# Expert weights in a two-block network: who makes the second parts of streamed weights, and how the spread weights lie in PSUM

## The chip, the cores and the metric

One core of one Trainium2 chip runs the whole program in one launch. The metric is device time in microseconds (us), the median of several runs. "PE" is TensorE, "DVE" VectorE, "ACT" ScalarE, "POOL" GpSimd, "SP" the engine whose queue issues most DMAs.

## The reference

The network takes 256 tokens of 1024 features through two layers of a first block (a mixer, then a layer of experts) and two layers of a second block (attention). The change lies in the experts. Each layer has 16384 experts; every token has 8 heads, each head picks 16 experts, and the output is the sum over the picked experts. Cut to that:

```python
def block(xb):
    q = (xb @ w_q).reshape(n, PEER_HEADS, 2, PEER_HALF)
    s = jnp.einsum('nhpc,pkc->nhpk', q, sk)
    sv, si = lax.top_k(s, PEER_TOPK)
    ...                                    # fv, eid: the 16 best pairs of each head
    gw = jax.nn.softmax(fv, axis=-1)
    u = u_tab[eid]
    act = jax.nn.gelu(jnp.einsum('nhkd,nd->nhk', u, xb), approximate=False)
    coef = gw * act
    return jnp.einsum('nhk,nhkd->nd', coef, v_tab[eid])
```

## The kernel before

**Dense experts.** The kernel gathers nothing. It computes the activation of every expert for every token (`u_pair`: gelu of u times x), multiplies it with a weight that is zero for experts that were not picked, and adds up all experts' outputs (`v_pairs`). Experts lie in 128 blocks of 128; a "pair" is two blocks and one DMA of 1 MB. The activations of 96 blocks lie in SBUF in three tiles `H[0]` to `H[2]`, each 128 partitions x 32 blocks x 256 tokens; they are a ring, so the u pairs and v pairs of `peer` are interleaved: u 0 to 47, v 0 to 7, u 48 to 55, v 8 to 15, u 56 to 63, v 16 to 63.

**Two parts of every number.** Weights are float32 and TensorE multiplies a shorter format (float32r). So `load_w` takes each 1 MB chunk `raw` in two halves: ScalarE copies a half to `whi` (line 122, the first part), and another engine subtracts `whi` from `raw` to make `wlo` (line 126, the second part). Each half then gives 24 products: 16 with `whi`, 8 with `wlo`. `whi` and `wlo` have 3 buffers each, `raw` has 3. The letter `lo` says which engine makes `wlo`: "p" GpSimd, "v" VectorE, "m" GpSimd for every third half and VectorE for the others.

**Spreading the weights.** `gates` takes 8 tokens and 64 blocks of experts at a time. A picked expert has a number within its block and a block number. VectorE compares both with a row of counts: `oh_b` (line 931, 128 x 1024 float16) and `oh_a` (line 934, 128 x 512), and multiplies `oh_a` with the softmax weights in two float16 parts: `oh_w` (line 938, two instructions). TensorE then makes, for each of the 8 tokens, `oh_b` times `oh_w` of both parts into 64 columns of a PSUM bank (line 942, 16 products of 64 columns), and VectorE multiplies the bank into two of the `H` tiles (line 949, two SCALAR_TENSOR_TENSOR instructions of 256 elements each). One call is made for each of 32 groups of tokens and each half of the blocks. The calls of the first half stand beside u pairs 32 to 46, those of the second beside v pairs 16 to 30, two calls (near the end three) to a pair. With two layers there are four such stages and 128 calls.

**Order.** A planner in the language's runtime orders the instructions of each engine from the order in which they are traced; waits between engines are semaphores that it places. `oh_b`, `oh_a` and `oh_w` have two buffers each, the PSUM banks named "tr" two. Side work for the second block (`beside`: lines 1065 to 1109, products of `w_ada` on VectorE) is spread over the experts' pairs too.

Of the kernel before, what the change touches and what calls it, by code (L numbers as in the profile page):

```python
# [20 lines left out]
P = 128  # L21
# [4 lines left out]
ALPHA = 4.0 ** 0.25  # L26
NEG = -1e30
LOWEST = -3.4e38
# the columns of a tile of tokens that are ready in turn
PIECES = (((0, 512), (512, 1024)), ((0, 512), (512, 768), (768, 1024)))  # L30
GATE_SCALE = 2.0 ** 14


def weave(main, fill, ratio):
    """Trace main, with ratio steps of fill to each of its own; then the rest of fill."""
    acc = 0.0
    for _ in main:
        acc += ratio
        while acc >= 1.0:
            next(fill, None)  # L40
            acc -= 1.0
    for _ in fill:
        pass
# [8 lines left out]
class Net:  # L52
# [8 lines left out]
    def new_T(self):  # L61
        """The slot of the features of the tokens: features on partitions, two parts."""
        return self.state.tile([P, KD, 2, S], F32R, name="xT", tag="xT", bufs=1)
# [13 lines left out]
    def consts(self, tmp):  # L77
# [5 lines left out]
        # row r, column c: NEG where c > r  # L83
# [12 lines left out]
    def mlstm_consts(self, c, d):  # L96
        """By row r and column k: 1 where r <= k; NEG where k < r; selectors of the heads' rows."""
# [10 lines left out]
    def load_w(self, src, width, nsub, lo="v", into=None):  # L108
        """The parts of a chunk of weights, of two products of the same columns; into: where to lay them."""
# [4 lines left out]
        parts = []  # L114
# [23 lines left out]
    def gemm_b(self, xT, chunk, ps, lo="m", KT=KD, fresh=False):  # L138
        """ps[:, 2, 256] <- (two blocks of 128 columns of W)^T x^T; a step is a block. fresh: x's
        second parts come last, in the first block."""  # L140
# [12 lines left out]
    def gemm_a(self, xT, chunks, ktc, w, evac, nsub=2, lo="m", ahead=False, tag="mm"):  # L153
        """evac(t, ps) with ps = x W for the two tiles of tokens, w columns; a step is a part of a
        chunk. ahead: the first tile's last products come before the second's."""
# [31 lines left out]
    def to_T(self, dst, t, src, k0, n, pin=False):  # L187
        """dst[:, k0:k0+n, hi|lo, tile t] <- src[:, t, blocks k0 to k0+n] transposed; pin: not
        ahead of what was traced before."""
        for k in range(k0, k0 + n, 4):  # L190
            m = min(4, k0 + n - k)
            self.split(*self.both(dst, t, k, m), self.turned(src[:, t], k, m, pin))
# [12 lines left out]
    def tokens_T(self, pool, dst, src, warm):  # L205
        """dst <- src transposed. The first tile's turn, which runs beside the second's norm, leaves
        VectorE alone."""
# [11 lines left out]
    def keep_warm(self, n):  # L219
        """Products that nobody reads, for a wait that would cost the tensor engine its clock."""  # L220
# [5 lines left out]
    def rstd(self, pool, var, eps, shape, more=None, before=None):  # L226
        """1 / sqrt(var + eps (+ more)): a first guess from the bits of the number, then a step of the
        third order and one of the second."""
# [19 lines left out]
        # 8 / 3 of the next guess, r (15 - 10 y + 3 y^2) / 8  # L248
# [6 lines left out]
    def refine_exp(self, e, sg):  # L255
        """e = exp(x) to float32's accuracy from the tables' exp(x) and sigmoid(x), x <= 0:
        one step towards e (1 - sg) = sg. sg is overwritten."""
# [13 lines left out]
    def stats(self, pool):  # L271
        """bn_stats of each piece of each tile of tokens."""
        return [pool.tile([P, len(PIECES[t]), 6], F32, name=f"ln_st{t}") for t in range(NT)]

    def layer_norm(self, pool, x, st, g, b):
        """x, one tile of tokens, in place; st: bn_stats of its pieces."""
# [4 lines left out]
        # (mean - x) g, so that the other factor is negative  # L281
# [9 lines left out]
    def add_norm(self, pool, x, t, i, ps, st, g, b, scale=ALPHA):  # L291
        """x <- scale x + ps, piece i of a tile of tokens; with the last piece the tile's norm."""
# [10 lines left out]
    def project(self, xT, src, order, evac, tags, store=None, late=3):  # L303
        """evac(t, i, ps) with ps = x W for a tile of tokens and piece i of the columns; src(n, i): the
        i-th half of W's rows, by blocks in this order, for 512 columns. The last products of a tile come
        together, of as many parts of W as late; three parts lie in the usual place, more in store."""
# [38 lines left out]
    def log1p_exp(self, pool, out, x, shape, tag):  # L345
        """out = log(1 + exp(x)), as max(x, 0) + 2 atanh(e / (2 + e)), e = exp(-|x|)."""
# [28 lines left out]
    def mem_kv(self, l, memT):  # L375
        """Keys of the memory, feature-major, and its values."""
# [10 lines left out]
    def feature_gemm(self, xT, chunk, dst, func=AF.Copy, scale=1.0, lo="m", fresh=False):  # L387
        """dst[:, 512] <- func(scale (two blocks of 128 columns of W)^T x^T)"""
# [53 lines left out]
    def mlstm(self, pool, x, xT, mixT, memT):  # L442
        nc, a = self.nc, self.a
        # gates
# [24 lines left out]
        # nB = -(running sum of the log forget gates); r = i - B  # L469
# [25 lines left out]
        # decay weights, transposed: [s, l]; columns: s0 x (l0, l1), s1 x l1  # L495
# [30 lines left out]
        # values (with a column of ones)  # L526
# [8 lines left out]
        # sigmoid(o) = (1 + tanh(o / 2)) / 2, with the norm's gain  # L535
# [17 lines left out]
        for c in range(2):  # L553
# [3 lines left out]
            if c:  # L557
                # beside the transposes of the first two heads
# [46 lines left out]
    def rglru(self, pool, own, xT, mixT):  # L605
# [34 lines left out]
        # softplus(-lam), times 4  # L640
# [22 lines left out]
        def recurrence():  # L663
            # sigmoid(z) = (1 + tanh(z / 2)) / 2
            for c in range(3):
# [12 lines left out]
                # 1 - a^2 = tanh(-log a) (1 + a^2); a half of its root  # L678
# [29 lines left out]
    def exp_neg(self, x, k, r):  # L708
        """x <- exp(x), x <= 0, on the vector engine alone: 2^k times a series in what is left.
        k and r are overwritten."""  # L710
# [23 lines left out]
    def peer(self, l, x1, beside, rate):  # L734
        """x1 <- layer_norm(ALPHA x1 + y); beside: steps that may run beside the products, at a rate
        for each pair of blocks."""
        nc, a, tc = self.nc, self.a, self.tc
        with ExitStack() as st:
            big = st.enter_context(tc.tile_pool(name=f"peer{l}", bufs=1, reuse_waits="tile"))
            # a ring of 96 blocks of experts' activations; the last two thirds are freed early  # L740
# [52 lines left out]
            if l:  # L793
                # the diagonals of the second block's gates
# [22 lines left out]
    def route(self, pool, H, l, xT, R):  # L817
        """The 16 experts of each head and token, and their weights, with the slots on partitions.
        What is needed here only lies in the part of H that is written last."""
# [53 lines left out]
        # softmax over the 16  # L873
# [9 lines left out]
        # the two halves of the expert's number  # L883
# [27 lines left out]
    def u_pair(self, l, xT, H, c):  # L911
        ps = self.bank("aux")
        yield from self.gemm_b(xT, self.a["u"][l, c], ps, "p" if c < 14 or 32 <= c < 48 else "m")
# [6 lines left out]
    def gates(self, pool, R, H, half, n):  # L920
        """H[64 blocks of this half, 8 tokens] *= the experts' weights, as two float16 parts,
        which carry all of float32's bits: the weights lie in 0..1, and are scaled away from the smallest.
        Tokens lie in pairs, so that all operands run through memory in steps of one."""
# [15 lines left out]
        g = self.bank("tr")  # L939
        for t in range(8):  # L940
            for k in range(2):
                i = nc.tensor.matmul(g[:, t * 64:(t + 1) * 64], B[:, t // 2, :, t % 2], W[:, k, t // 2, :, t % 2],  # L942
# [3 lines left out]
        gv = g.rearrange("p (t i) -> p t i", t=8)  # L946
        for i0, hh in ((0, H[2 * half]), (32, H[1 - half])):
            h = hh[:, :, ts].rearrange("p i t -> p t i")
            nc.vector.scalar_tensor_tensor(out=h, in0=gv[:, :, i0:i0 + 32], scalar=1.0 / GATE_SCALE, in1=h,  # L949
                                           op0=OP.mult, op1=OP.mult)  # L950

    def v_pairs(self, pool, l, H, c0, c1):
        """y += the experts' outputs, two blocks of experts in a step."""
        for c in range(c0, c1):
            ch, cl = (pool.tile([P, 2 * S], F32R, name=n, tag=n, bufs=2) for n in ("ch", "cl"))
            self.split(ch, cl, self.h_pair(H, c))
            parts = self.load_w(self.a["v"][l, c], 2048, 2, "p" if 16 <= c < 32 else "v" if c >= 48 else "m")
# [6 lines left out]
    def v_products(self, t, out, first, last, b, ch, cl, hi, lw):  # L964
        """out: (first and last column, where) of each part."""
# [8 lines left out]
    def v_tail(self, pool, l, H, c0, done):  # L974
        """The last experts' outputs, tile by tile, from operands that are all laid ready; the steps lay
        them, a pair of blocks each. done(t, ys) with the sums of those before,
        done(t, y, i) with what piece i adds."""
# [44 lines left out]
    def load_T(self, pool, name, dst, parts):  # L1022
        """Features on partitions from DRAM, in two parts."""
# [8 lines left out]
    def bias_tables(self, pool):  # L1032
        """Rows of bias over distance, written 128 times, so that a pitch of one less skews them."""
# [19 lines left out]
    def bias_ap(self, h, off):  # L1053
        """The three groups' biases of a head for queries off tiles after the keys."""
# [4 lines left out]
    def rope_tables(self, pool):  # L1059
        """cos and sin of positions * inv_freq, by token."""  # L1060
# [29 lines left out]
    def modulation(self, pool, l, thirds):  # L1090
        """By feature: the shift, norm_g (1 + scale) and a half of the gate."""
# [22 lines left out]
    def gate_rows(self, l):  # L1114
        """The gate along the free dimension, on all partitions. Returns what is still to be done."""
# [10 lines left out]
    def rms_of(self, pool, ms):  # L1126
        """1 / sqrt(mean(x^2) + eps); the mean is the sum of ms' columns."""
# [7 lines left out]
    def rms(self, pool, srcs, tag):  # L1135
        """1 / sqrt(mean(x^2) + eps) of each of srcs, [P, len(srcs)]."""
# [12 lines left out]
    def second_layer(self, l, x, stats):  # L1149
        """x <- x + ..., and the result after the last layer; stats: the mean squares of x's pieces by  # L1150
        tile, or None. Returns those of the new x."""
        nc, a, tc = self.nc, self.a, self.tc
        mod = self.mods[l]
        with ExitStack() as st:
# [36 lines left out]
            # latents of the second mixer  # L1191
# [5 lines left out]
            # twice silu(z) = z (1 + tanh(z / 2))  # L1197
# [26 lines left out]
            # twice sigmoid(z) = 1 + tanh(z / 2)  # L1224
# [62 lines left out]
    def softmax_parts(self, pool, p, mx, parts):  # L1287
        """exp(s - max) / sum, of parts (t, columns) of p."""
# [9 lines left out]
    def dilated(self, l, pool, dil, Q, za, yaT):  # L1298
        """yaT <- the first mixer, gated; the three groups of a head are one softmax. v holds a half."""
# [8 lines left out]
        def scores(h, bias):  # L1308
            r = slice((h % 2) * 64, (h % 2) * 64 + 64)
            # columns: (tile of queries, tile of keys) = (0, 0), (1, 0), (1, 1), by groups  # L1310
# [373 lines left out]
```

## Time and profile before

| | |
|---|---|
| median of 3 runs | 2968.83 us (2956.13 to 2976.85) |
| profiled execution, span from first to last instruction | 2973.3 us |
| TensorE busy / VectorE busy / GpSimd busy | 91% / 64% / 41% of the span |
| mean granted TensorE clock | 0.948 |
| stages in which weights are spread | 467 to 614, 857 to 994, 1584 to 1731, 1909 to 2046 us |

No time of the profiled execution is given beside its span; the span lies 4.5 us above the median and within the runs' spread. Busy shares are means over stages with different limits; the four stages of the last row have to be read by themselves. A TensorE instruction's mean duration is its latency in a pipeline; the cost of one in a row of many is the step from start to start.

### The profile page before, as it was taken

To read this page: it belongs to the slowest core of one execution; us is meant where nothing else is said; L and a number is where in the kernel's file an instruction comes from. 1 tells how busy PE (TensorE), PEld (TensorE's weight loads), DVE (VectorE), ACT (ScalarE), POOL (GpSimd) and SP (SyncE) were. 2 spreads that over 40 slices of the span, in tenths; PEclk is the share of its full clock that TensorE was granted. 3 is DMA by queue.
4 is the path that set the end of the run, shared out by engine and by line. 5 is a ranking of instruction groups with operands and counts; after the bars stand their busy time and mean duration, and the time that the engine had idled before them with its cause. 6 is when DMAs were issued, how large, how long until landed. Compare 5 with 4: busy or idle time off the path is not lost.

```text
span 2973.3 us, 46557 instructions
## 1 busy us (share of the span) xinstructions
PE 2716.6 (91%) x18920; PEld 2440.4 (82%) x18920; DVE 1908.7 (64%) x3423; ACT 1257.7 (42%) x1724; POOL 1214.8 (41%) x587
## 2 busy tenths in 40 slices
PE   8899798899588999889798899989999999999998
PEld 7789798888576787789798788867878988889888
DVE  5678947963259656879858963487566345564455
ACT  4544343343233453634342244423545554455544
POOL 3348535622157413348436622484223321143212
PEclk9999898899789999889898899999999999999999
DMA  5334365345743455234475455424553444443443
GB/s 201 117 139 165 137 241 185 123 158 170 130 161 114 157 208 186 100 115 171 144 259 172 169 213 176 179 100 156 190 187 114 146 156 131 137 150 134 166 130 102
DMA packets 90915, 467.42 MB, mean 157 GB/s; under 512 B 14627, under 2 KB 27171, under 8 KB 42316
## 3 DMA queue, kind: packets, MB, share of 16 engines
q1 hardware_dynamic: 86188, 459.44, 43.9%
q0 software_dynamic: 4224, 4.74, 1.8%
q8 instruction: 148, 2.42, 0.3%
q14 instruction: 67, 0.55, 0.1%
q10 hardware_dynamic: 288, 0.26, 0.0%
HBM read 458.62 MB, written 5.75 MB: 156 GB/s over the span
## 4 chain that ended last, share of the span: by engine, by line
PE 59%; DVE 27%; DMA 7%; issue 3%; ACT 2%; POOL 2%; SPq 0%; ACTq 0%; DVEq 0%; POOLq 0%
PE mm L150 15%; PE aux L150 12%; PE mm L970 11%; PE mm L972 5%; DVE oh_w L938 4%; DVE H L949 3%; DVE oh_b L931 3%; DMA raw<-in_v 2%; DMA w_ada<-in_w_adaT 2%; DVE wlo L126 2%; PE mm L136 2%; POOL wlo L126 2%; PE mm L135 2%; PE mm L134 2%; DMA skew<-rows 1%
## 5 line engine op out<-in xcount | busy, mean ns | idle before, releaser
L126 POOL TENSOR_TENSOR wlo<-raw,whi 128x1024 fp32r<-128x1024 f32 (+2 forms) x408 | 1103.0, 2714 | 1491.8 <-ACT whi L122 1366.3
L122 ACT ACTIVATE whi<-raw 128x1024 fp32r<-128x1024 f32 (+3 forms) x795 | 821.2, 1035 | 1208.2 <-PE aux L150 509.1
L126 DVE TENSOR_TENSOR wlo<-raw,whi 128x1024 fp32r<-128x1024 f32 (+3 forms) x387 | 491.4, 1274 | 443.4 <-ACT whi L122 415.8
L150 PE MATMUL aux<-xT,whi 128*128 128x256 f32 x4096 | 565.3, 293 | 30.7 <-ACT H L914 15.5
L150 PEld LDWEIGHTS aux<-xT,whi 128*128 128x128 f32 x4096 | 537.7, 202 | 32.5 <-ACT H L914 16.5
L150 PE MATMUL mm<-xT,whi 128*128 128x256 f32 x2624 | 369.4, 292 | 1.3 <-ACT xT L184 0.9
L150 PEld LDWEIGHTS mm<-xT,whi 128*128 128x128 f32 x2624 | 338.5, 195 | 10.3 <-issue 4.0
L970 PE MATMUL mm<-wlo,ch 128*128 128x512 f32 x976 | 315.3, 405 | 17.7 <-POOL wlo L126 12.5
L970 PE MATMUL mm<-whi,ch 128*128 128x512 f32 x976 | 316.0, 406 | 5.7 <-ACT whi L122 5.7
L972 PE MATMUL mm<-whi,cl 128*128 128x512 f32 x976 | 312.4, 401 | 0.0
L150 PE MATMUL aux<-xT,wlo 128*128 128x256 f32 x2048 | 291.0, 285 | 0.0
L150 PEld LDWEIGHTS aux<-xT,wlo 128*128 128x128 f32 x2048 | 268.0, 194 | 0.1
L970 PEld LDWEIGHTS mm<-wlo,ch 128*128 128x128 f32 x976 | 186.7, 193 | 69.4 <-POOL wlo L126 17.3
L185 DVE TENSOR_TENSOR cl<-H,ch 128x512 fp32r<-128x512 f32 x128 | 127.5, 1001 | 180.2 <-ACT ch L184 179.9
L972 PEld LDWEIGHTS mm<-whi,cl 128*128 128x128 f32 x976 | 188.1, 193 | 44.8 <-DVE cl L185 0.4
L970 PEld LDWEIGHTS mm<-whi,ch 128*128 128x128 f32 x976 | 185.0, 193 | 48.4 <-ACT whi L122 6.3
L150 PE MATMUL mm<-xT,wlo 128*128 128x256 f32 x1312 | 189.6, 287 | 0.9 <-POOL wlo L126 0.9
L942 PE MATMUL tr<-oh_w,oh_b 128*128 128x64 f16 x2048 | 98.3, 204 | 88.5 <-DVE oh_w L938 85.2
L150 PEld LDWEIGHTS mm<-xT,wlo 128*128 128x128 f32 x1312 | 173.7, 196 | 2.2 <-POOL wlo L126 1.1
L942 PEld LDWEIGHTS <-oh_b 128*128 128x128 f16 x2048 | 80.7, 104 | 111.8 <-DVE oh_w L938 68.9
L949 DVE SCALAR_TENSOR_TENSOR H<-tr,H 128x256 f32<-128x256 f32 x256 | 163.1, 703 | 9.2 <-PE tr L942 9.2
L938 DVE TENSOR_TENSOR oh_w<-oh_a,gk 128x512 f16<-128x512 f16 x256 | 168.4, 696 | 0.0
(680 smaller groups left out, 3256.2 us busy)
## 6 DMA issues: line engine op xcount, KB each, us to landing
raw<-in_u SPq DMA_DIRECT2D x128, 1024.0 KB, 4.8
raw<-in_v SPq DMA_DIRECT2D x128, 1024.0 KB, 4.8
w_ada<-in_w_adaT SPq DMA_DIRECT2D x48, 512.0 KB, 3.8
raw<-in_w_q SPq DMA_DIRECT2D x16, 1024.0 KB, 4.8
raw<-in_in_mg SPq DMA_DIRECT2D x16, 1024.0 KB, 4.9
raw<-in_in_q SPq DMA_DIRECT2D x12, 1024.0 KB, 4.8
raw<-in_in_k SPq DMA_DIRECT2D x12, 1024.0 KB, 4.8
raw<-in_in_v SPq DMA_DIRECT2D x12, 1024.0 KB, 4.8
```

The source lines that it names most:

```text
L122: nc.scalar.activation(hi[:, :n], r, AF.Copy)
L126: i = e.tensor_sub(lw[:, :n], r, hi[:, :n].bitcast(F32))
L134: mm(ps, lh, rh, start=first, stop=False)
L135: mm(ps, ll, rh, start=False, stop=False)
L150: mm(o, w[:, k * P:(k + 1) * P], xT[:, k, p], start=i == 0, stop=i == 3 * KT - 1)
L185: self.nc.vector.tensor_sub(lo, src, hi.bitcast(F32))
L931: nc.vector.tensor_tensor(out=B, in0=self.iota2[:, None].to_broadcast([P, 4, P, 2]), in1=by_pair(slotT[:, 1, ts], P), op=OP.is_equal)
L938: nc.vector.tensor_tensor(out=W[:, k], in0=A, in1=by_pair(gk[:, k, ts], 64), op=OP.mult)
L942: i = nc.tensor.matmul(g[:, t * 64:(t + 1) * 64], B[:, t // 2, :, t % 2], W[:, k, t // 2, :, t % 2], start=k == 0, stop=k == 1)
L949: nc.vector.scalar_tensor_tensor(out=h, in0=gv[:, :, i0:i0 + 32], scalar=1.0 / GATE_SCALE, in1=h, op0=OP.mult, op1=OP.mult)
L970: mm(y, ch[:, s], w[:, c0:c1], start=first and w is hi, stop=False)
L972: mm(y, cl[:, s], hi[:, c0:c1], start=False, stop=last)
```

## The change

Three edits. In `u_pair`, pairs 32 to 47 take letter "v" in place of "p"; in `v_pairs`, pairs 16 to 31 do the same; so VectorE makes all `wlo` of the four stages and GpSimd none. In `gates`, the PSUM bank is laid out with the 8 tokens innermost: TensorE writes the 64 columns of one token 8 words (32 bytes) apart, where they lay side by side before. VectorE's last two instructions then run through the bank in steps of one, and through `H` in runs of 8 tokens side by side with 1 KB from run to run; before, they ran through `H` with 1 KB from every element to the next.

```diff
     def u_pair(self, l, xT, H, c):
-        yield from self.gemm_b(xT, self.a["u"][l, c], ps, "p" if c < 14 or 32 <= c < 48 else "m")
+        yield from self.gemm_b(xT, self.a["u"][l, c], ps, "p" if c < 14 else "v" if 32 <= c < 48 else "m")
...
-        g = self.bank("tr")
+        g = self.bank("tr").rearrange("p (i t) -> p i t", t=8)
         for t in range(8):
             for k in range(2):
-                i = nc.tensor.matmul(g[:, t * 64:(t + 1) * 64], B[:, t // 2, :, t % 2], W[:, k, t // 2, :, t % 2],
+                i = nc.tensor.matmul(g[:, :, t], B[:, t // 2, :, t % 2], W[:, k, t // 2, :, t % 2],
                                      start=k == 0, stop=k == 1)
...
-        gv = g.rearrange("p (t i) -> p t i", t=8)
         for i0, hh in ((0, H[2 * half]), (32, H[1 - half])):
-            h = hh[:, :, ts].rearrange("p i t -> p t i")
-            nc.vector.scalar_tensor_tensor(out=h, in0=gv[:, :, i0:i0 + 32], scalar=1.0 / GATE_SCALE, in1=h,
+            h = hh[:, :, ts]
+            nc.vector.scalar_tensor_tensor(out=h, in0=g[:, i0:i0 + 32], scalar=1.0 / GATE_SCALE, in1=h,
                                            op0=OP.mult, op1=OP.mult)
...
-            parts = self.load_w(self.a["v"][l, c], 2048, 2, "p" if 16 <= c < 32 else "v" if c >= 48 else "m")
+            parts = self.load_w(self.a["v"][l, c], 2048, 2, "v" if 16 <= c < 32 or c >= 48 else "m")
```

The diff also takes out comments, which leave blank lines; line numbers stay nearly the same.

## Rows read from the trace of the kernel before

**Rows 1.** Busy time by stage: us, PE, PEld, DVE, ACT, POOL, PEclk, DMA, GB/s.

```profile
467.00:614.00 147.00, 120.31 (x1235) 115.96 (x1234) 135.08 (x210) 42.22 (x50) 81.26 (x29) 0.87 0.36 127
857.00:994.00 137.00, 113.76 (x880) 89.34 (x879) 130.09 (x199) 40.06 (x46) 97.64 (x29) 0.91 0.33 119
1584.00:1731.00 147.00, 124.05 (x1160) 117.89 (x1160) 145.68 (x218) 41.34 (x48) 86.72 (x27) 0.87 0.45 155
1909.00:2046.00 137.00, 114.70 (x879) 89.88 (x879) 119.74 (x197) 40.38 (x46) 98.16 (x30) 0.91 0.33 120
sum 568.00, PE 472.82 PEld 413.08 DVE 530.59 ACT 164.00 POOL 363.77; mean PE 118.21 PEld 103.27 DVE 132.65 ACT 41.00 POOL 90.94
```

**Rows 2.** Waits of the first stage, 467 to 614: total, times, longest.

```profile
PE tr L942 <- DVE oh_w L938: 25.7, 14, 4.2
```

**Rows 3.** Groups of the first stage: count | busy us, mean ns | idle before.

```profile
L126 POOL TENSOR_TENSOR wlo<-raw,whi 128x1024 fp32r<-128x1024 f32 x29 | 83.1, 2880 | 55.5 <-ACT whi L122 40.3 <-PE aux L150 14.9
...
L938 DVE TENSOR_TENSOR oh_w<-oh_a,gk 128x512 f16<-128x512 f16 x60 | 43.8, 769 | 0.0
...
L931 DVE TENSOR_TENSOR oh_b<-iota,slotT 128x1024 f16<-128x1024 f16 x31 | 30.3, 979 | 0.0
...
L1104 DVE CUSTOM_DVE_ANT_0 w_ada<-w_ada,act 128x1024 f32<-128x1024 f32 x5 | 8.2, 1636 | 8.0 <-DMA w_ada<-in_w_adaT 8.0
```

**Rows 4.** Tile oh_w over the whole span: duration ns min/median/max.

```profile
L942 PE MATMUL tr<-oh_w,oh_b x2048: 189/193/242, 467.6 to 2044.3; 128*128 128x64 f16 x187
L938 DVE TENSOR_TENSOR oh_w<-oh_a,gk x256: 404/411/2622, 362.4 to 2043.4; 128x512 f16<-128x512 f16 x128
```

**Rows 5.** Timeline of DVE, 520 to 538: start us, us, what.

```profile
520.47 0.75 DVE L934 TENSOR_TENSOR oh_a<-iota,slotT 128x512 f16<-128x512 f16 x2
521.14 0.17 DVE L1084 TENSOR_SCALAR angk<-ang 128x32 f32<-128x32 f32 x1
...
532.95 2.46 DVE L949 SCALAR_TENSOR_TENSOR H<-tr,H 128x256 f32<-128x256 f32 x4
535.30 0.70 DVE L931 TENSOR_TENSOR oh_b<-iota,slotT 128x1024 f16<-128x1024 f16 x1
535.90 0.77 DVE L938 TENSOR_TENSOR oh_w<-oh_a,gk 128x512 f16<-128x512 f16 x2
536.57 0.70 DVE L931 TENSOR_TENSOR oh_b<-iota,slotT 128x1024 f16<-128x1024 f16 x1
```

**Rows 6.** Timeline of DVE, 355 to 366.

```profile
361.29 1.22 DVE L126 TENSOR_TENSOR wlo<-raw,whi 128x1024 fp32r<-128x1024 f32 x1 [0.99 <-PE aux L150]
362.43 0.75 DVE L938 TENSOR_TENSOR oh_w<-oh_a,gk 128x512 f16<-128x512 f16 x2
```

**Rows 7.** Groups of DVE by shape, whole span: three that read PSUM.

```profile
L949 DVE SCALAR_TENSOR_TENSOR H<-tr,H 128x256 f32<-128x256 f32 x256 | 163.1, 703 | 9.2 <-PE tr L942 9.2
...
L1464 DVE TENSOR_TENSOR zm<-o,zm 128x256 f32<-128x256 f32 x16 | 6.8, 424 | 31.4 <-PE o L1461 31.4
...
L1207 DVE SCALAR_TENSOR_TENSOR zm<-zm,mm 128x512 f32<-128x512 f32 x8 | 5.4, 681 | 4.0 <-ACT zm L1206 4.0
```

**Rows 8.** Groups of the third stage, 1584 to 1731.

```profile
L1104 DVE CUSTOM_DVE_ANT_0 w_ada<-w_ada,act 128x1024 f32<-128x1024 f32 x16 | 19.4, 1213 | 0.0
```

**Rows 9.** Groups of the second stage, 857 to 994.

```profile
L185 DVE TENSOR_TENSOR cl<-H,ch 128x512 fp32r<-128x512 f32 x15 | 19.3, 1284 | 18.5 <-ACT ch L184 18.4
```

**Rows 10.** Timeline of PE, 408 to 440, products of u (start us, us, what).

```profile
409.98 2.08 PE L150 MATMUL aux<-xT,whi 128*128 128x256 f32 x16
...
412.86 2.08 PE L150 MATMUL aux<-xT,whi 128*128 128x256 f32 x16
```

**Rows 11.** Timeline of PE, 960 to 985: products of v, then spread weights.

```profile
965.41 0.62 PE L972 MATMUL mm<-whi,cl 128*128 128x512 f32 x2
965.88 1.14 PE L942 MATMUL tr<-oh_w,oh_b 128*128 128x64 f16 x32
966.86 0.71 PE L970 MATMUL mm<-whi,ch 128*128 128x512 f32 x2
```

## The prediction

> **What bounds the kernel now.** TensorE is busy for 91% of the span, but the change touches four stages of 568 us in all, so the view to read first is busy time by stage [rows 1]. There VectorE, not TensorE, is the fullest engine: 530.6 us of 568, and in the third stage 145.7 of 147. Next, the waits of one stage: TensorE stands waiting 25.7 us of the first stage for `oh_w` [rows 2], and its granted clock is 0.87 there. So these stages end when VectorE is done with spreading, and what the change is worth is what it does to VectorE's 530.6 us, as long as TensorE doesn't become the longer one.
>
> Why is VectorE so long? Its groups [rows 3] against its best instructions [rows 4]: `oh_w` takes 411 ns at the median and 769 ns in the mean of this stage, with single ones of 2622 ns. The long ones are as long as one GpSimd subtraction, 2880 ns in this stage [rows 3]; I read them as VectorE held until GpSimd's subtraction ends. That hold is what the first edits take away, and they pay for it with more work for VectorE.
>
> **The change part by part.** All steps are from start to start in stretches in which nothing is held.
>
> *One call of gates today.* `oh_b` 535.90 - 535.30 = 0.60 us; two `oh_w` 536.57 - 535.90 = 0.67; `oh_a` half of 521.14 - 520.47, 0.335; two line 949 half of 535.30 - 532.95, 1.175 [rows 5]. Sum 2.78 us.
>
> *Line 949 after.* It keeps its 256 elements; what changes is that `H` is read and written in runs of eight. Today it takes 703 ns, and a subtraction step in PSUM and SBUF of the same size that runs side by side takes 424 [rows 7]; 512 side by side of the same operation take 681, so one element costs (681 - 424) / 256 = 1.0 ns, and the 279 ns between 703 and 424 are a second such step per element, for the 1 KB hops. No row shows runs of eight, so the bounds are 424 and 703. I take 424, since seven hops of eight are gone; less the overlap with the next one (703 - 588 = 115 ns [rows 5, 7]) that is a step of 0.31 us. A call is then 0.60 + 0.67 + 0.335 + 0.62 = 2.225 us, 0.55 less. [...]
>
> *wlo on VectorE.* One costs 362.43 - 361.29 = 1.14 us [rows 6]. GpSimd makes 29, 29, 27 and 30 in the stages [rows 1, 3]: some 115 go over, 131 us of new work for VectorE. ScalarE, the DMA queue and `raw` keep their work; GpSimd gets idle, and has nothing else in these stages, so no hold is left.
>
> *The hold.* What goes is `oh_w`, `oh_b`, `w_ada` and `cl` beyond their own durations: in the first stage 60 x (0.769 - 0.411) = 21 us, 31 x (0.979 - 0.69) = 9 us [rows 3 to 5], and 5 x (1.636 - 1.213) = 2 [rows 3, 8]; in the second `cl` alone 15 x (1.284 - 0.68) = 9 [rows 9], where 0.68 is what 512 elements take [rows 7].
>
> *VectorE's sum by stage.* First: 32 calls 71.2 + 31 wlo (29 and the two it makes already) 35.3 + `w_ada` 5.8 + small side work 2 = 114. Third: 30 calls 66.8 + 30 wlo 34.2 + 16 `w_ada` 19.4 [rows 8] + some `cl` 2 = 122. Second and fourth: 71.2 + 35.3 + 14 or 15 `cl` 9 = 116 each. Together 468 against 530.6: the hold and line 949 give back more than the 131 us cost.
>
> *TensorE.* A half of u takes 412.86 - 409.98 = 2.88 us for 24 products [rows 10]; 16 for v go at 0.47 per two [rows 11]; the 32 spreading products take 966.86 - 965.88 = 0.98 us, 31 ns each [rows 11]. The first stage has 1235 - 512 = 723 other products, 723 x 0.12 = 87 us, and the third, with a few of v, 90; the second and fourth 368 x 0.233 = 86. That is 348 us, and 512 + 512 + 448 + 512 = 1984 spreading products at 31 ns add 62: 410 in all, below VectorE's 468.
>
> *The price of spread columns* is unknown: every TensorE output in the trace lies side by side. Below: 31 ns, no cost (a gain has no reason, the same columns are written). Above: each spread column costs what four side by side do, so 64 cost as 256, 0.12 us [rows 10]. I take something up to 0.06, nearest to rows of the same shape; then TensorE has 348 + 1984 x 0.062 = 471, level with VectorE.
>
> First the row: 64 columns at 31 ns each product [rows 11]. [...]
>
> *Sum.* VectorE's idle in the stages was 568 - 530.6 = 37. If it stays, the stages take 468 + 37 = 505, 63 less. But VectorE is now one queue for two things that TensorE wants in turn: a `wlo` queues behind `oh_w`, the spreading behind `wlo` (which itself waits for ScalarE's `whi`, and that for a buffer that TensorE frees). With TensorE at 410 to 471 beside 468, such waits have less slack; I put 4 us a stage, 16 in all, an estimate of the order of the longest wait today [rows 2]. That leaves -47: profiled 2973.3 to 2926, and from the median, 4.5 lower and equal within its spread, 2968.8 - 47 = **2922 us**. After the stages the order is unchanged; nothing collides later.
>
> **The rivals.**
> *Spread columns are dear.* TensorE becomes the bound. With 37 us of idle as now, the stages take 348 + 37 + 1984 p; that equals 568 at p = 0.092 us, and is over by 1% from 0.108. At the upper bound of 0.12 it is 623: 2969 + 55 = 3024, slower. [...] Against it: today's product of 64 columns is already far from the cost of its 193 ns latency [rows 4], and it takes a price of more than three times.
> *VectorE stays the end.* If line 949 keeps 703 ns, 252 x 0.28 = 70 us come back on VectorE: 468 + 70 + 37 = 575, and the time is 2976, no change. A price of 0.08 to 0.10 on TensorE, or queueing of 12 us a stage more than I put, gives the same answer. For it: VectorE carries 131 us of new work in a single queue. Against it: two elements' time for one is just what hops explain [rows 7].
> *All hides.* The idle shrinks with the hold, TensorE's clock rises: 468 + 10 = 478, -90, 2879 us.
> That the edits don't do what they say can't be: `wlo` is the only work of GpSimd in these stages [rows 1, 3].
>
> **How the numbers follow.** About 1%, 30 us, is what a measurement of this kernel can tell from no change. Forecast, with gains of 30 to 75: 0.52. All hides: 0.08. VectorE stays or the price is in the middle: 0.25. Dear columns: 0.15, nearly all over 1%. So faster 0.60, same 0.25, slower 0.15. The range runs from 2872, below the full gain, to 2990, over the no-change case and its spread, and leaves out the dear columns and little else.
>
> **What the changed profile would show.** Line 949 near 420 ns; `oh_w` at 411 in the mean too; 115 more `wlo` on VectorE at 1.22; no GpSimd in the stages; bursts of 32 spreading products in 0.98 us if columns cost nothing, 2 at 0.062, 3.8 at 0.12; the stages at some 130 and 128 us. The prediction fails if those bursts take over 3 us, or if line 949 stays near 700, or if TensorE waits for `wlo` as long as it did for `oh_w`.

## The result and the profile after

The changed kernel takes 2885.36 us (median of 4 runs, 2883.12 to 2888.77) against 2972.84 us for the kernel before on the same chip: ratio 0.9727, 95% interval 0.9695 to 0.9759. That is 87 us less, where I had forecast 47 less. The profiled execution has a span of 2884.6 us and took 2886.36.

Busy time by stage after the change (columns as in [rows 1]). The windows lie near the first and the last spreading product, not on them: the third one before begins 13 us behind its first product (at 1570.74), the third one after 6.6 us ahead of its own (at 1521.58).

```profile
462.00:580.00 118.00, 116.82 (x1234) 115.40 (x1234) 107.16 (x217) 40.25 (x48) 0.00 (x0) 1.00 0.41 147
822.00:940.00 118.00, 113.33 (x838) 89.25 (x835) 108.97 (x222) 36.76 (x42) 0.00 (x0) 1.00 0.35 125
1515.00:1640.00 125.00, 124.60 (x1294) 122.94 (x1293) 113.41 (x224) 44.51 (x52) 0.68 (x1) 1.00 0.42 152
1833.00:1957.00 124.00, 119.33 (x875) 94.17 (x874) 112.61 (x226) 39.76 (x45) 0.00 (x0) 1.00 0.35 121
sum 485.00, PE 474.08 PEld 421.76 DVE 442.15 ACT 161.27 POOL 0.68; mean PE 118.52 PEld 105.44 DVE 110.54 ACT 40.32 POOL 0.17
```

The four windows took 568 us [rows 1] and take 485, 83 of the 89 us by which the span fell; from the first to the last spreading product the stages took 557 us and take 466. What the reader is to see is which column is full. Before it was VectorE's (530.6 of 568), now it is TensorE's: 474.1 of 485, with VectorE at 442. GpSimd is out of the stages. And TensorE's granted clock is 1.00 in all four, where it was 0.87 and 0.91, and TensorE hardly waits any more (11 of 485 us). Its busy time is the same as before (472.8), though its spreading products became dearer. What they cost more was gained elsewhere: in the kernel before, 90 of TensorE's 473 us of work in the stages fell into slices of 1 us with a granted clock of 0.50, and after the change no slice of them does. One such place, behind a wait for `oh_w` in its first stage:

```profile
532.07 1.29 PE L942 MATMUL tr<-oh_w,oh_b 128*128 128x64 f16 x16 [2.47 <-DVE oh_w L938]
533.17 3.76 PE L150 MATMUL aux<-xT,whi 128*128 128x256 f32 x16
536.73 1.75 PE L150 MATMUL aux<-xT,wlo 128*128 128x256 f32 x8
```

Behind a wait of 2.47 us, 16 products of u take 536.73 - 533.17 = 3.56 us, and the granted clock from 533 to 537 is 0.50. The same 16 take 505.75 - 503.75 = 2.00 us in the timeline of the changed kernel below, at a granted clock of 1.00. Over the whole span TensorE's busy time didn't change (2716.6 us before, 2715.7 after) and VectorE's fell by 30 us (1908.7 to 1879.0): the 89 us are nearly all TensorE's idle time.

The tile `oh_w` over the whole span (duration ns min/median/max), and the tile `H`'s row of the step that multiplies by the weights:

```profile
L942 PE MATMUL tr<-oh_w,oh_b x2048: 216/247/247, 462.2 to 1954.2; 128*128 128x64 f16 x187
L938 DVE TENSOR_TENSOR oh_w<-oh_a,gk x256: 407/415/2629, 356.9 to 1953.0; 128x512 f16<-128x512 f16 x128
```

```profile
L948 DVE SCALAR_TENSOR_TENSOR H<-tr,H x256: 408/414/427, 468.5 to 1955.4; 128x256 f32<-128x256 f32 x128
```

The last step fell from 703 ns in the mean to 414 at the median [rows 7], the spreading product rose from 193 to 247 ns [rows 4]. What it costs in a row of many is the step in the timeline of TensorE:

```profile
501.98 1.96 PE L942 MATMUL tr<-oh_w,oh_b 128*128 128x64 f16 x32
503.75 2.16 PE L150 MATMUL aux<-xT,whi 128*128 128x256 f32 x16
505.75 1.12 PE L150 MATMUL aux<-xT,wlo 128*128 128x256 f32 x8
506.71 2.08 PE L150 MATMUL aux<-xT,whi 128*128 128x256 f32 x16
508.63 1.12 PE L150 MATMUL aux<-xT,wlo 128*128 128x256 f32 x8
509.59 1.96 PE L942 MATMUL tr<-oh_w,oh_b 128*128 128x64 f16 x32
```

32 products take 503.75 - 501.98 = 1.77 us, 55 ns each, where it was 0.98 us [rows 11]. From burst to burst it is 7.61 us, and no idle time stands between: 5.84 for the two halves of u and 1.77 for spreading. The chain of waits of the first stage says the same, with TensorE on nearly all of it:

```profile
by line: PE aux L150 68.8%; PE tr L942 22.3%; DMA w_ada<-in_w_adaT 3.6%; issue 1.9%; DVE H L948 1.2%; DVE oh_w L938 1.1%; DVE oh_b L931 1.0%; DVE w_ada L1103 0.1%; DVE mod L1103 0.1%; DVE wlo L126 0.0%; DVEq L1103 0.0%
```

And in the waits of that stage, the 25.7 us for `oh_w` [rows 2] are 1.0:

```profile
PE tr L942 <- DVE oh_w L938: 1.0, 1, 1.0
```

### The profile page after: what moved, and what is told of

It is laid out like the page before. It is cut to its first block, busy times and chain, and to the rows that moved or that the text cites. A ratio compares the mean times of both kernels' runs of the same rounds, so it can differ in the third digit from the quotient of the medians.

```text
span 2884.6 us, 46516 instructions
## 1 busy us (share of the span) xinstructions
PE 2715.7 (94%) x18920; PEld 2445.2 (85%) x18920; DVE 1879.0 (65%) x3551; ACT 1257.7 (44%) x1724; POOL 813.7 (28%) x459
## 4 chain that ended last, share of the span: by engine, by line
PE 67%; DVE 18%; DMA 9%; issue 3%; ACT 2%; POOL 0%; SPq 0%; DVEq 0%; ACTq 0%; POOLq 0%
PE mm L150 16%; PE aux L150 14%; PE mm L969 12%; PE mm L971 6%; DMA w_ada<-in_w_adaT 4%; PE tr L942 3%; DVE wlo L126 3%; DMA raw<-in_v 2%; PE mm L136 2%; PE mm L135 2%; PE mm L134 2%; DMA skew<-rows 1%; PE aux L1316 1%; DMA raw<-in_u 1%; DVE H L894 1%
## 5 line engine op out<-in xcount | busy, mean ns | idle before, releaser
L126 POOL TENSOR_TENSOR wlo<-raw,whi 128x1024 fp32r<-128x1024 f32 (+1 forms) x280 | 703.0, 2516 | 1805.9 <-ACT whi L122 1716.4
L126 DVE TENSOR_TENSOR wlo<-raw,whi 128x1024 fp32r<-128x1024 f32 (+3 forms) x515 | 657.5, 1282 | 424.3 <-ACT whi L122 393.5
L150 PE MATMUL aux<-xT,whi 128*128 128x256 f32 x4096 | 549.0, 288 | 29.8 <-ACT H L914 15.0
L150 PEld LDWEIGHTS aux<-xT,whi 128*128 128x128 f32 x4096 | 522.0, 196 | 31.7 <-ACT H L914 16.0
L185 DVE TENSOR_TENSOR cl<-H,ch 128x512 fp32r<-128x512 f32 x128 | 118.3, 926 | 116.0 <-ACT ch L184 115.9
L184 ACT ACTIVATE ch<-H 128x512 fp32r<-128x512 f32 x128 | 80.2, 631 | 145.2 <-PE mm L969 133.4
L942 PEld LDWEIGHTS <-oh_b 128*128 128x128 f16 x2048 | 117.2, 122 | 28.9 <-issue 14.2
L942 PE MATMUL tr<-oh_w,oh_b 128*128 128x64 f16 x2048 | 136.0, 246 | 5.7 <-DVE oh_w L938 3.8
L1103 DVE CUSTOM_DVE_ANT_0 w_ada<-w_ada,act 128x1024 f32<-128x1024 f32 x48 | 68.3, 1423 | 93.6 <-DMA w_ada<-in_w_adaT 93.6
```

What stands on the lines that cost most here:

```text
L126: i = e.tensor_sub(lw[:, :n], r, hi[:, :n].bitcast(F32))
L150: mm(o, w[:, k * P:(k + 1) * P], xT[:, k, p], start=i == 0, stop=i == 3 * KT - 1)
L184: self.nc.scalar.activation(hi, src, AF.Copy)
L185: self.nc.vector.tensor_sub(lo, src, hi.bitcast(F32))
L942: i = nc.tensor.matmul(g[:, :, t], B[:, t // 2, :, t % 2], W[:, k, t // 2, :, t % 2], start=k == 0, stop=k == 1)
L1103: nc.vector.tensor_tensor_reduce(r, r, self.act, 1.0, 0.0, OP.mult, OP.add, v[:, k:k + 1])
```

## The experiments

**The two halves by themselves.** Theory A: the hold goes with the letters, the hops with the layout, and both are needed to bring VectorE below TensorE. Rivals: the hold alone (B), the layout alone (C). The first kernel has the letters alone:

```diff
 # kernel before
-    "p" if c < 14 or 32 <= c < 48 else "m"                 # u_pair
+    "p" if c < 14 else "v" if 32 <= c < 48 else "m"
-    "p" if 16 <= c < 32 else "v" if c >= 48 else "m"       # v_pairs
+    "v" if 16 <= c < 32 or c >= 48 else "m"
```

> VectorE makes wlo in the four stages, but the spread weights lie token by token as before, so line 949 keeps its hops of 1 KB. Theory A (both halves are needed: the hold goes with the first edits, the hops with the last, and only together does VectorE fall below TensorE): VectorE's sum is 468 + 70 = 538 us plus some 20 us of idle, so the stages take some 555 of 568 us and the time is 2945 to 2970 us; oh_w near 0.41 us in the mean, line 949 at 0.70 us. Rival B (the hold alone was the cost): 2885 to 2905 us. Rival C (the layout alone does it): 2970 us or more.

2928.45 us against 2969.95, ratio 0.9845 (0.9823 to 0.9867): 41 us less, between theory A and rival B, and more than A gave. VectorE's timeline shows a pair of u:

```profile
501.31 0.69 DVE L931 TENSOR_TENSOR oh_b<-iota,slotT 128x1024 f16<-128x1024 f16 x1
501.91 0.76 DVE L938 TENSOR_TENSOR oh_w<-oh_a,gk 128x512 f16<-128x512 f16 x2
502.58 0.69 DVE L931 TENSOR_TENSOR oh_b<-iota,slotT 128x1024 f16<-128x1024 f16 x1
503.18 0.77 DVE L938 TENSOR_TENSOR oh_w<-oh_a,gk 128x512 f16<-128x512 f16 x2
503.85 1.23 DVE L126 TENSOR_TENSOR wlo<-raw,whi 128x1024 fp32r<-128x1024 f32 x1
504.99 0.76 DVE L934 TENSOR_TENSOR oh_a<-iota,slotT 128x512 f16<-128x512 f16 x2
505.66 1.23 DVE L126 TENSOR_TENSOR wlo<-raw,whi 128x1024 fp32r<-128x1024 f32 x1
506.79 2.57 DVE L949 SCALAR_TENSOR_TENSOR H<-tr,H 128x256 f32<-128x256 f32 x4
509.26 0.70 DVE L931 TENSOR_TENSOR oh_b<-iota,slotT 128x1024 f16<-128x1024 f16 x1
```

No gap and nothing held: VectorE is the end, with 509.26 - 501.31 = 7.95 us a pair, of which line 949 has 2.47. In its four stages VectorE is busy for 504 of 513 us. My A was too high in both terms: I let 20 us of idle stand, and 9 are left; and the 538 us of work had 25 of `w_ada` in it, of which 6 are left in the stages. Over the whole span VectorE even works longer than before, 1931.9 us for 1908.7: `wlo` takes 166 us more, and `oh_w`, `oh_b` and `cl` give back 108. So the letters alone gain by waits that are gone, not by less work for VectorE.

The other half, the layout with GpSimd's letters left as before:

```diff
 # changed kernel
-    "p" if c < 14 else "v" if 32 <= c < 48 else "m"        # u_pair
+    "p" if c < 14 or 32 <= c < 48 else "m"
-    "v" if 16 <= c < 32 or c >= 48 else "m"                # v_pairs
+    "p" if 16 <= c < 32 else "v" if c >= 48 else "m"
```

> The spread weights lie with eight tokens side by side, but GpSimd keeps all wlo of the four stages. Theory A: VectorE's sum is 530 - 70 = 460 us, and its hold by GpSimd stays, so VectorE is still the end in part: 2905 to 2935 us, oh_w at 0.6 us or more in the mean. Rival B (hold alone): 2960 us or more. Rival C (layout alone): 2885 to 2895 us.

2962.23 us, ratio 0.9975 (0.9958 to 0.9992): 8 us less; A's 35 to 65 were wrong. The halves bring 41 and 8 us, both together 87. The groups of VectorE (busy us, mean ns) show where it went:

```profile
L938 DVE TENSOR_TENSOR oh_w<-oh_a,gk 128x512 f16<-128x512 f16 x256 | 174.4, 720 | 0.0
...
L934 DVE TENSOR_TENSOR oh_a<-iota,slotT 128x512 f16<-128x512 f16 x128 | 103.3, 843 | 0.1
L948 DVE SCALAR_TENSOR_TENSOR H<-tr,H 128x256 f32<-128x256 f32 x256 | 92.0, 413 | 15.2 <-PE tr L942 13.8
```

The last step is at 413 ns, 71 us less busy in all [rows 7]; but `oh_a`, 432 ns in the changed kernel, takes 843 here, and `oh_w` 720. Is it this hold that ate the 71 us, or TensorE's dearer products? The same letters with cheap products (the layout of the next experiment) tell:

> TensorE writes side by side and VectorE reads PSUM in hops (line 948 at 0.42 us, no price on TensorE), but GpSimd makes all wlo of the four stages, as in the kernel before. If the layout alone brought so little because of the spread columns' 49 us on TensorE, this gives them back: 2915 to 2935 us. If it is the hold that eats what line 948 saves, since VectorE comes back to the next float16 instruction sooner while GpSimd is still at work: 2945 to 2965 us, with oh_a, oh_b, oh_w and cl together held some 200 us in all.

2966.61 us, ratio 0.9981 (0.9963 to 0.9998), 2 us above the range that I gave for the hold and far from the other one: it is the hold. `oh_w` is at 822 ns there and `oh_a` at 637. Side by side, the timelines of VectorE and of GpSimd in this run:

```profile
535.36 0.68 DVE L931 TENSOR_TENSOR oh_b<-iota,slotT 128x1024 f16<-128x1024 f16 x1
535.96 2.96 DVE L938 TENSOR_TENSOR oh_w<-oh_a,gk 128x512 f16<-128x512 f16 x2
538.84 2.95 DVE L934 TENSOR_TENSOR oh_a<-iota,slotT 128x512 f16<-128x512 f16 x2
541.71 1.41 DVE L948 SCALAR_TENSOR_TENSOR H<-tr,H 128x256 f32<-128x256 f32 x4
```

```profile
535.76 2.54 POOL L126 TENSOR_TENSOR wlo<-raw,whi 128x1024 fp32r<-128x1024 f32 x1 [1.55 <-ACT whi L122]
538.63 2.54 POOL L126 TENSOR_TENSOR wlo<-raw,whi 128x1024 fp32r<-128x1024 f32 x1 [0.33 <-ACT whi L122]
```

Two `oh_w`, which need 0.75 us for both, start with a subtraction of GpSimd and end after it (538.30 for GpSimd, 538.92 for them), and two `oh_a` do the same with the next one (541.17, 541.79). Line 948 takes its own time, 411 ns in the mean over the span. So in this stretch GpSimd's subtractions and these float16 instructions go one after the other. Over the span line 948 takes 72 us less than line 949 did before (90.6 for 163.1), and `oh_w`, `oh_a` and `oh_b` take 63 us more.

**Which side of the hop costs what.** TensorE writes side by side again, and VectorE reads the bank in hops of 64 words, still in runs of eight through `H`:

```diff
 # changed kernel
-        g = self.bank("tr").rearrange("p (i t) -> p i t", t=8)
+        g = self.bank("tr").rearrange("p (t i) -> p i t", t=8)
```

> As the changed kernel, but TensorE writes a token's 64 columns side by side again, and VectorE reads the bank in hops of 64 words while it goes through H in runs of eight tokens. If a hop costs VectorE the same in PSUM as in SBUF, line 948 takes 0.65 to 0.70 us and the time is that of the letters alone, 2945 to 2970 us. If hops in PSUM cost VectorE nothing, line 948 stays at 0.42 us, the 32 spreading products fall from 1.77 to 0.98 us, and the time is 2850 to 2875 us, for TensorE is the end of the stages and gets back up to 1984 x 24 ns = 48 us.

2853.46 us, ratio 0.9605 (0.9582 to 0.9627). Hops in PSUM cost VectorE nothing that can be told, 417 ns in the mean for 416 in the changed kernel, in its groups:

```profile
L948 DVE SCALAR_TENSOR_TENSOR H<-tr,H 128x256 f32<-128x256 f32 x256 | 93.0, 417 | 6.4 <-PE tr L942 6.0
```

Now both engines are full. Its first stage:

```profile
458.00:566.00 108.00, 106.05 (x1241) 104.31 (x1240) 106.40 (x217) 41.33 (x49) 0.89 (x1) 1.00 0.45 157
```

TensorE has 106.05 of 108 us and VectorE 106.40. Timed again beside the changed kernel on one chip:

> The fastest so far once more, on the same chip as the changed kernel: 2845 to 2862 us, about 1.1% below the changed kernel, as TensorE's 32 spreading products take 0.98 us in place of 1.77.

> The changed kernel itself, beside the one above: 2880 to 2892 us.

2852.82 us (ratio 0.9611, 0.9574 to 0.9648) and 2881.82 us (0.9702, 0.9664 to 0.9741): 29 us, or 1.0%, are the price of the spread columns, and this version beats both kernels. It is less than 1984 x 24 ns = 48 us; I put that down to VectorE, which becomes full on the way, but no run shows it by itself.

What makes a spread column dear? One kernel with two layouts, its bank read as in the changed kernel, so that the weights come out permuted:

```diff
 # changed kernel; b is the bank
+        out = ((lambda t: b.rearrange("p (q i e) -> p q i e", i=64, e=2)[:, t // 2, :, t % 2]) if layer
+               else (lambda t: b.rearrange("p (c t r) -> p c t r", t=8, r=2)[:, :, t]))
-                i = nc.tensor.matmul(g[:, :, t], ...
+                i = nc.tensor.matmul(out(t), ...
```

> As the changed kernel, VectorE reads the bank in the same order, but TensorE lays the columns of a token in pairs of neighbours (layer 0) or two words apart (layer 1), so the weights come out permuted among experts and tokens. If a column by itself in its pair of words is what costs, layer 0 falls to some 31 ns a spreading product and layer 1 stays at some 55 ns. If any hop costs, both stay at 55. If the length of the hop counts, layer 1 is cheaper than 55.

The timeline of TensorE, first in layer 0 (neighbours in pairs, 16 words from pair to pair), then in layer 1 (each column two words from the next):

```profile
505.36 1.15 PE L945 MATMUL tr<-oh_w,oh_b 128*128 128x64 f16 x32
506.34 2.15 PE L150 MATMUL aux<-xT,whi 128*128 128x256 f32 x16
...
1563.69 1.96 PE L945 MATMUL tr<-oh_w,oh_b 128*128 128x64 f16 x32
1565.47 2.16 PE L150 MATMUL aux<-xT,whi 128*128 128x256 f32 x16
```

0.98 us with pairs, as if all lay side by side; 1.78 us two words apart, the same as eight words apart (in the changed kernel a burst reads 1.96 us long in layer 1 too, at 1521.58, so it isn't the layer). So in these layouts it counts whether the columns lie in pairs, and not how long the hop is: without pairs a product takes 55 ns for 31. One run took 2864.70 us.

**The hold by itself.** The rival to it was that GpSimd's `wlo` came late to TensorE. The waits over the whole span of the kernel before speak against it:

```profile
PE tr L942 <- DVE oh_w L938: 85.2, 46, 4.2
PE mm L970 <- POOL wlo L126: 12.5, 9, 2.5
```

In the fastest version, GpSimd now does work whose result nobody reads: in the four stages each half of a chunk starts, through a ScalarE copy of one column into it, a subtraction of a tile `idle` of 128 x 1024.

```diff
 # fastest version; "d" is the letter of u 32 to 47 and v 16 to 31, made on VectorE
+            if on == "d":
+                nc.scalar.activation(self.idle[:, :1], r[:, :1], AF.Copy)
+                nc.gpsimd.tensor_sub(self.idle, self.idle, self.idle)
```

> As the fastest so far; VectorE makes all wlo, and GpSimd does a subtraction of 128 x 1024 on a tile that nobody reads for each of them, started by a ScalarE copy of one column. Hold theory (GpSimd's work holds VectorE, whatever it is for): each costs VectorE some 1.2 us, as in the kernel before (35 us a stage for 29), so 128 cost 100 to 155 us: 2940 to 3010 us. Rival (GpSimd's wlo came late to TensorE, and that was the cost): 2850 to 2870 us, since nobody waits for these.

In the next, `nc.gpsimd.memset(self.idle, 0.0)` stands in place of the subtraction, which writes SBUF and reads nothing; and in the last one nothing, so only ScalarE's copies are left.

> As the run with the idle subtractions, but GpSimd fills the tile with zeros instead: it writes SBUF and reads nothing. If VectorE is held only while GpSimd reads SBUF: 2850 to 2870 us and no instruction of VectorE over its own duration. If any work of GpSimd holds it: more, in proportion to the fill's length.

> As the run with the idle fills, with ScalarE's copies of one column and the idle tile, but GpSimd does nothing in the stages. If the 18 us that the fills cost are ScalarE's copies and their place in the order: 2865 to 2875 us, as with the fills. If the fills themselves held VectorE: 2850 to 2860 us, as without them.

The subtractions: 3027.70 us (ratio 1.0174, 1.0137 to 1.0211), slower than the kernel before. The fills: 2871.18 (0.9656, 0.9624 to 0.9688). The copies alone: 2869.44 (0.9655, 0.9614 to 0.9695). Against the copies, 128 subtractions cost 158 us, 1.24 us each, and 128 fills nothing that can be told. GpSimd's groups and VectorE's, of the subtractions and then of the fills (in these kernels `oh_w` is line 948, `oh_b` line 941, and the last step line 958):

```profile
L128 POOL TENSOR_TENSOR idle<-idle 128x1024 f32<-128x1024 f32 x128 | 310.8, 2428 | 290.1 <-ACT idle L127 289.8 <-PE aux L153 0.3
...
L948 DVE TENSOR_TENSOR oh_w<-oh_a,gk 128x512 f16<-128x512 f16 x256 | 139.3, 577 | 0.0
L941 DVE TENSOR_TENSOR oh_b<-iota,slotT 128x1024 f16<-128x1024 f16 x128 | 112.1, 876 | 0.0
```

```profile
L128 POOL MEMSET idle<- 128x1024 f32 x128 | 122.1, 954 | 318.2 <-ACT idle L127 318.2
...
L948 DVE TENSOR_TENSOR oh_w<-oh_a,gk 128x512 f16<-128x512 f16 x256 | 107.2, 455 | 0.0
L941 DVE TENSOR_TENSOR oh_b<-iota,slotT 128x1024 f16<-128x1024 f16 x128 | 87.9, 686 | 0.0
```

With the copies alone `oh_w` is at 449 ns, `oh_b` at 680. So GpSimd's subtraction, which reads SBUF, holds VectorE though nobody uses its result, and the fill, which only writes, doesn't (`oh_w` 455 ns, `oh_b` 686). Longer beside the subtractions than beside the copies are VectorE's instructions with two inputs in SBUF: `oh_b`, `oh_w`, `oh_a` (457 ns for 415), `wlo` (1401 for 1302) and `cl` (961 for 938). Line 958 has one input there and the other in PSUM, and is at 412 ns for 414.

The 158 us are not the hold alone. All subtractions use one tile, so ScalarE's next copy waits until the last one is done with it, and `whi` comes behind that copy:

```profile
ACT idle L127 <- POOL idle L128: 182.0, 67, 5.9
```

With the fills it is 64.3 us. VectorE's busy time over the span is 123 us higher with the subtractions than with the copies (1995.1 for 1872.5), 0.96 us for each; the rest of the 1.24 is time in which VectorE waits. Why the copies by themselves cost some 16 us against the fastest version stays open.

**A third on GpSimd.** Does a little help pay? In the fastest version both letters of the stages are "m":

> As the fastest so far (side by side in PSUM, VectorE hops), but GpSimd makes every third wlo of the four stages. If the hold is what GpSimd's work costs, 10 subtractions a stage save VectorE 11 us and hold it for 10 to 24 us, with no slack left beside TensorE: 2860 to 2900 us. If GpSimd's help is worth more than its hold: 2835 to 2850 us.

2877.39 us (0.9675, 0.9642 to 0.9708), 24 us more than with none (21 by the ratios, as the chip was another). `oh_b` is at 965 ns in the mean there. GpSimd has 298 subtractions of this shape in place of 254, which is 44 x 1.14 = 50 us less `wlo` for VectorE; but its busy time over the span fell only from 1869.3 to 1863.3, so the hold took nearly all of it back.

## Why the prediction came out as it did

- *VectorE ends the stages.* Borne out for the kernel before: with the letters alone VectorE is full (7.95 us a pair), and idle subtractions, which lengthen its instructions (`oh_w` from 449 to 577 ns), lengthen the time, from 2869 to 3028 us. After the change it is wrong; see the sum.
- *The hold goes with GpSimd's work.* Right, and shown: `oh_w` is at 441 ns in the mean over the span, where it was 696, and 128 idle subtractions bring it up again, from 449 to 577.
- *Line 949 at 424, 0.31 a step.* Right: 414 ns, a step of 0.33 (in the changed kernel four start at 503.46 and the next instruction at 504.78). (The row of 424 that it was taken from is a multiplication, not a subtraction; the number holds.) That it was the hops through `H` and not through PSUM is shown by the reading in hops, 417 ns.
- *wlo, 115 over, 131 us.* 128 went over (some lay outside the stages' bounds), and over the span VectorE's time on `wlo` rose by 166 us (467.0 to 633.1), while `oh_w`, line 949, `oh_b` and `cl` fell by 64 + 69 + 33 + 9. "Give back more than they cost" held, narrowly, and only with line 949: the letters alone give back 108 for 166.
- *The price of spread columns, up to 0.06.* No run shows the 0.062 us of the sum, twice the row's 31 ns, nor the 0.12 above it; the runs showed 0.055 in their place. So the bound was right, and TensorE has 348 + 1984 x 0.055 = 457 us of work. (1984 leaves out 64 products that stand ahead of the third window; they add 4 us.)
- *The sum, 468 + 37 + 16.* Here is the miss in size, and a step of the mechanism that failed: that VectorE stays the end, with its old idle and new queueing on top. The stages were forecast at 521 us and measured 485, and these 36 us are nearly all of the 40 by which the forecast was too small. After the change TensorE is the end; it stands idle for 11 of 485 us. In the terms of the sum, VectorE's work was put at 468 and measured 442, 26 too high, and some 20 of these are `w_ada`. I counted the 21 products that stood in the stages before [rows 3, 8] at 25 us; 4 are left, in the first and in the third stage:

```profile
L1103 DVE CUSTOM_DVE_ANT_0 w_ada<-w_ada,act 128x1024 f32<-128x1024 f32 x1 | 1.2, 1227 | 2.1 <-DMA w_ada<-in_w_adaT 2.1
...
L1103 DVE CUSTOM_DVE_ANT_0 w_ada<-w_ada,act 128x1024 f32<-128x1024 f32 x3 | 3.7, 1226 | 7.4 <-DMA w_ada<-in_w_adaT 7.4
```

The others run outside the stages now, most of them behind the third one: 18 of all 48 stand between 1640 and 1760. The remaining 10 us are waiting: VectorE's idle is 485 - 442 = 43 us, where I put 37 + 16. So the old idle did stay in size, but beside a full TensorE it no longer sets the time. Why `w_ada` moved, and which of the old waits went with the hold, no experiment took apart.

- *The rivals.* "All hides" (2879) came nearest in time and had 0.08, but by luck: it wanted VectorE full with 468 us of work and 10 of idle, and measured are 442 and 43. "Dear columns" named the engine that ends the stages now, TensorE; its loss is excluded by 55 ns, below the 0.092 us from which it begins.
- *Which part did it.* I had added the two gains. They don't add: 41 and 8 us apart, 87 together, since the letters alone leave VectorE full and the layout alone leaves the hold.

## What to carry to other kernels

When one engine holds another, count the waits behind the hold and not only the held time: a subtraction on VectorE cost 1.14 us there, and an idle one on GpSimd made VectorE's work 0.96 us longer, so by work alone the move doesn't pay; it paid by the waits that went. Look for a layout's cost on each side by itself: hops were dear for VectorE in SBUF (703 ns for 416) and for TensorE's writes in single words (55 ns for 31), and free for VectorE's reads from PSUM (417 ns for 416), so in this kernel the hop belongs there. And when two engines come out level, don't add the old idle time of the one that was the end; take the larger of the two sums first. Here the 471 us of TensorE were nearer to the 485 measured than VectorE's 468 with 53 on top.

## What the runs showed that I had not expected

VectorE reads float32 from PSUM 64 words apart at 417 ns for 256 elements, as fast as side by side (416), while the same 256 elements with hops of 1 KB through SBUF take 703. And TensorE's price of 24 ns on 64 columns is gone as soon as columns lie in pairs (0.98 us for 32 products against 1.78 at two words).
